# Weight preparation three chunks ahead instead of two, in the mixers of a two-layer block

## The chip, the core and the metric

The kernel runs on one core of a Trainium2 chip. The metric is the device time of one execution in microseconds (us), and the median of several executions is compared. The profile names the engines PE (TensorE matmul), PEld (its weight loads), DVE (VectorE), ACT (ScalarE), POOL (GpSimd) and SP (the engine that issues most DMA transfers).

## The reference

Two layers (`DEPTH = 2`) work on 256 tokens of width 1024. Each layer is a half FFN, a mixer and another half FFN, all in float32:

```python
for l in range(DEPTH):
    x = x + 0.5 * swiglu(rms_norm(x, norm_ffn1[l]), ffn1_wi[l], ffn1_wo[l])
    h = rms_norm(x, norm_mix[l])
    (u, q_raw, k_cmp, v_cmp, k_sel, v_sel, k_win, v_win,
     nsa_gate, gate_a, gate_b) = jnp.split(h @ w_in[l], SPLIT_POINTS, axis=-1)
    y_a = s5_branch(u, ...)            # a linear state-space scan over the tokens, then a gated product
    y_b = nsa_branch(q_raw, ...) @ nsa_w_up[l]   # attention over compressed, selected and window keys
    merged = jax.nn.sigmoid(gate_a) * y_a + jax.nn.sigmoid(gate_b) * y_b
    x = x + merged @ w_out[l]
    x = x + 0.5 * swiglu(rms_norm(x, norm_ffn2[l]), ffn2_wi[l], ffn2_wo[l])
```

The FFN's inner width is 2816. The columns of `w_in` are 512 for u, 512 for q, six groups of 128 for keys and values, 24 gate logits, and 1024 each for gate_a and gate_b.

## The kernel before, in words

**Weights come in chunks.** `plan` lists every chunk of weights of the whole program in the order of use, each 128 partitions by at most 1024 columns. A chunk is loaded into a buffer `raw` (four of them, `nr`), and then split: ScalarE writes a high part `whi` (L169 with the norm's gain as a scale, L349 without), and VectorE the low part `wlo` as the rest (L170, L349). There are four `whi` and four `wlo` buffers (`nh`). The chunks of `w_in`, which this text speaks of most, hold two blocks of 128 rows and are split in two halves, so two instructions on each engine for a chunk. Every product is made of three matmuls (`mm3`, L381 to L383): high by high, high by the activation's low part, low by high.

**How far ahead a split stands.** `next` hands out the next chunk and first calls `prepare` with a distance, `LA` = 2. `prepare` emits splits (and the loads that they need) until that many chunks beyond the one handed out are split:

```python
        while k.ns < min(k.nu + la, n):
```

Here `ns` counts the chunks split and `nu` those handed out.

**A mixer's work in order** (`mix`). A `gemm` makes a product of 256 tokens by up to 512 columns: two banks of PSUM with the tag `gu`, one for each half of the tokens (t), of which there are two in all; so the next `gemm` needs a bank that has been evacuated. The gemms are: u (512 columns, chunks in two pairs, each pair for both t), keys and values for the compression (384), the other keys and values with the gate logits (408), then two products with compression weights that stay in `raw` (L550 on the tile `kc`), q (512), four for the two gates (512 each, evacuated by a tanh at L1322), four with `ssm_w_glu`, two with `nsa_w_up`, and the output projection. The first evacuation of u is at L1282, and scales by the token's norm; VectorE transposes it (L1283), and the state-space branch starts from it (L550 on `ya` and `yb`, rotations at L933 to L941, the scan at L890, and the products with the state at L907). The evacuation of q is at L1049.

**The norm.** x is normed after the product: the hidden activations of the products are x itself, and each evacuation multiplies by the reciprocal root mean square. `norms` makes it, by a square with a running sum for each half of the tokens on ScalarE (L363) and two small steps on GpSimd. It is called behind the mixer's first gemm, and sets where ScalarE takes the two squares:

```python
        with k.tc.issue_after(k.hi_ins[k.ns - k.opt['SQ']].ins):
            k.rn = [k.rstd(t) for t in range(2)]
```

`SQ` is 1, so on ScalarE the squares stand behind the high part of the latest chunk that has been split. `hi_ins` holds each chunk's last high instruction.

**What sets the order.** The instructions are recorded in the order of the Python code, and a scheduler then sets each engine's own order by dependencies, free buffers, priorities and a model of the time. Each engine takes its instructions in that order. So a split that is emitted earlier moves other instructions around it on ScalarE, VectorE and TensorE.

Of the kernel before, what the change touches and what calls it, by code (L numbers as in the profile page):

```python
# [79 lines left out]
class Model:  # L80
    def __init__(k, tc, ctx, a, out, opt):
        k.tc, k.nc, k.a, k.out, k.opt = tc, tc.nc, a, out, opt
        e = ctx.enter_context
        k.pc = e(tc.tile_pool(name="const", bufs=1))
        k.pw = e(tc.tile_pool(name="weights", bufs=4))
        k.ps = e(tc.tile_pool(name="work", bufs=2))
        k.pp = e(tc.tile_pool(name="psum", bufs=1, space=PSUM))
        if not opt.get('auto', True):
            e(tc.manual_schedule())
        k.chunks, k.raw, k.hl, k.hi_ins = [], {}, {}, {}  # L90
        k.nd = k.ns = k.nu = k.held = 0
        k.bg, k.credit, k.budget = None, 0.0, 0.0
        k.fence, k.fence_n, k.late = (), 0, []
        k.steps = []


    def bank(k, shape=(128, 512), tag="tr", dtype=F32):
# [81 lines left out]
    def pull(k):  # L179
        k.credit = min(k.credit + k.budget, k.budget)  # L180
        while k.bg and k.credit > 0:
            cost = next(k.bg, None)
            if cost is None:
                k.bg = None
            else:
                k.credit -= cost

    def next(k, la=None):

        i = k.nu  # L190
        k.nu += 1
        if i and not k.chunks[i - 1][1]:
            k.held -= 1
        k.prepare(k.opt['LA'] if la is None else la)
        k.pull()
        return k.hl.pop(i)

# [1064 lines left out]
    def mix(k):  # L1262
# [2 lines left out]
        N = k.N  # L1265
        r4 = lambda dt=F32: k.sb([128, 1024], "r4", k.opt['n4'], dt)
        r8 = lambda: k.sb([128, 2048], "r8", k.opt['n8'])
        N['V'] = k.sb([128, 2, 2, 128], "V", 1)
        N['kT'] = k.sb([128, 2, 2, 2, 256], "kT", 1, F32R)
        ps = k.gemm(k.hstat, 8, 512, k.turns(k.opt['O2']))  # L1270
# [83 lines left out]
        def mm(kk, t, W, hs=(0, 1)):  # L1354
            for h in hs:
                cs = slice(h * 512, (h + 1) * 512)
                k.mm3(y[t, h], k.hstat(kk, t), (W[0][:, cs], W[1][:, cs]), kk == 0, kk == 7)

        for kk in range(5):
            W = k.next()  # L1360
            for t in range(2):
                mm(kk, t, W)
# [43 lines left out]
def hybrid_kernel(tc, out, opt, **a):  # L1406
    with ExitStack() as ctx:
# [3 lines left out]
_INS = ['x', 'norm_ffn1', 'ffn1_wi', 'ffn1_wo', 'norm_mix', 'w_in', 'ssm_lambda_re', 'ssm_lambda_im', 'ssm_log_dt',  # L1411
        'ssm_b_re', 'ssm_b_im', 'ssm_c_re', 'ssm_c_im', 'ssm_d', 'ssm_w_glu', 'q_norm', 'k_norm', 'cmp_pe', 'cmp_w1',
        'cmp_w2', 'nsa_w_up', 'w_out', 'norm_ffn2', 'ffn2_wi', 'ffn2_wo']
OPT = dict(nr=4, nh=4, LA=2, DLA=3, n1=10, n2=8, n4=7, n8=5, HP=2000, HN=2000, BG=1.2, FN=1, O1=22, WU=7, WV=7, SQ=1, LB=1, FB=2, O2=22, B1=1.0, B2=1.0)


# [17 lines left out]
```

## Time and profile before

| | us |
|---|---|
| median of 3 runs | 1166.65 (1166.4 to 1167.07) |
| the profiled execution | 1167.36 |
| its span, first to last instruction | 1165.6 |
| TensorE busy | 1153.3 (99% of the span) |
| VectorE busy | 827.1 (71%) |
| ScalarE busy | 671.9 (58%) |
| first mixer, 200.99 to 416.23 | 215.24 |
| second mixer, 779.03 to 991.47 | 212.44 |

The ends of matmuls are modelled and overlap the next matmul's start, so a busy TensorE says that something was always in flight, and the starts of the matmuls tell how fast they go. The two mixers are bounded here by the same two instructions of the program, the first update of x by the FFN ahead of them and a product at the same place of the FFN behind them.

### The profile page before, as it was taken

How to read it: one execution, taken by the hardware profiler on the slowest of the kernel's cores; microseconds unless marked ns; L12 is line 12 of the kernel's file. 1: busy time of each engine (PE TensorE's matmuls, PEld its weight loads, DVE VectorE, ACT ScalarE, POOL GpSimd, SP SyncE). 2: the span in 40 equal slices, each digit the busy share in tenths (PEclk: the TensorE clock that was granted, in tenths of full speed). 3: DMA queues.
4: the chain of work that ended last, by engine and by line, in shares of the span. 5: the costliest groups of instructions: out<-in, count | busy, mean ns of one | idle time of the engine just before them, and what ended most of it. 6: DMA issues, size and time to landing. Idle time of an engine off the chain costs nothing.

```text
span 1165.6 us, 17595 instructions
## 1 busy us (share of the span) xinstructions
PE 1153.3 (99%) x6148; PEld 939.7 (81%) x6148; DVE 827.1 (71%) x1578; ACT 671.9 (58%) x1176; POOL 96.0 (8%) x177
## 2 busy tenths in 40 slices
PE   9999999999999999999999999999999999999998
PEld 6888887877877888888888888788788778888886
DVE  5798597797776665555567986977987666655654
ACT  6755665646674565555566565555667646555552
POOL 3000000021032000000030000002112200000000
PEclk9999999999999999999999999999999999999999
DMA  8765646464443566665665555565654335766662
GB/s 239 232 193 166 186 144 209 124 204 141 155 118 106 174 206 191 187 183 185 192 181 184 181 179 169 157 178 158 200 162 145 109 110 170 227 184 185 191 183 88
DMA packets 150266, 200.40 MB, mean 172 GB/s; under 512 B 10145, under 2 KB 121025, under 8 KB 150177
## 3 DMA queue, kind: packets, MB, share of 16 engines
q1 hardware_dynamic: 148656, 196.93, 55.4%
q0 software_dynamic: 1136, 1.82, 0.8%
q8 instruction: 48, 0.79, 0.3%
q10 hardware_dynamic: 384, 0.52, 0.2%
q14 instruction: 42, 0.34, 0.1%
HBM read 198.18 MB, written 1.05 MB: 171 GB/s over the span
## 4 chain that ended last, share of the span: by engine, by line
PE 95%; DVE 3%; ACT 1%; issue 0%; POOL 0%; DVEq 0%; ACTq 0%; POOLq 0%
PE gu L381 20%; PE gu L383 20%; PE gu L382 20%; PE yb L382 4%; PE yb L383 4%; PE yb L381 4%; PE ya L383 4%; PE ya L381 4%; PE ya L382 4%; PE tr L496 2%; PE yb L1238 1%; PE yb L907 1%; PE tr L375 1%; PE tr L1227 1%; PE gu L448 1%; PE ya L1194 1%
## 5 line engine op out<-in xcount | busy, mean ns | idle before, releaser
L169 ACT ACTIVATE whi<-raw,gcol 128x512 fp32r<-128x512 f32 (+2 forms) x480 | 316.2, 710 | 197.8 <-PE gu L382 84.7
L170 DVE SCALAR_TENSOR_TENSOR wlo<-raw,gcol,whi 128x512 fp32r<-128x512 f32 (+2 forms) x480 | 335.6, 738 | 108.2 <-ACT whi L169 106.2
L381 PE MATMUL gu<-whi,hh 128*128 128x512 f32 (+2 forms) x944 | 373.5, 396 | 1.8 <-ACT r L1322 1.8
L383 PE MATMUL gu<-wlo,hh 128*128 128x512 f32 (+2 forms) x944 | 367.7, 393 | 0.0
L382 PE MATMUL gu<-whi,hl 128*128 128x512 f32 (+2 forms) x944 | 367.6, 389 | 0.0
L349 DVE TENSOR_TENSOR wlo<-raw,whi 128x1024 fp32r<-128x1024 f32 x128 | 156.5, 1225 | 120.0 <-ACT whi L349 117.2
L381 PEld LDWEIGHTS gu<-whi,hh 128*128 128x128 f32 x944 | 177.9, 188 | 36.3 <-ACT r L1322 2.6
L382 PEld LDWEIGHTS gu<-whi,hl 128*128 128x128 f32 x944 | 178.1, 189 | 34.8 <-issue 0.2
L383 PEld LDWEIGHTS gu<-wlo,hh 128*128 128x128 f32 x944 | 177.3, 188 | 34.8 <-issue 0.3
L349 ACT CAST whi<-raw 128x1024 fp32r<-128x1024 f32 x128 | 134.4, 1053 | 121.2 <-PE gu L382 102.4
L382 PE MATMUL yb<-whi,w1k 128*128 128x512 f32 x176 | 71.2, 406 | 0.2
L382 PE MATMUL ya<-whi,w1k 128*128 128x512 f32 x176 | 68.7, 392 | 0.0
L383 PE MATMUL yb<-wlo,w1k 128*128 128x512 f32 x176 | 68.1, 392 | 0.0
L381 PE MATMUL yb<-whi,w1k 128*128 128x512 f32 x176 | 68.0, 393 | 0.0
L381 PE MATMUL ya<-whi,w1k 128*128 128x512 f32 x176 | 67.6, 394 | 0.0
L383 PE MATMUL ya<-wlo,w1k 128*128 128x512 f32 x176 | 67.1, 390 | 0.0
L349 ACT CAST w1k<-tr 128x256 fp32r<-128x256 f32 x88 | 32.4, 368 | 43.5 <-PE tr L496 43.1
L513 DVE SCALAR_TENSOR_TENSOR w1k<-gu,rs,w1k 128x256 f32<-128x256 f32 x88 | 42.0, 479 | 16.8 <-ACT w1k L512 16.8
L512 ACT ACTIVATE w1k<-gu,rs 128x256 f32<-128x256 f32 x88 | 40.9, 467 | 18.4 <-PE gu L383 15.7
L356 POOL TENSOR_SCALAR rs<-ss 128x1 f32<-128x1 f32 (+3 forms) x22 | 6.8, 309 | 523.8 <-ACT w2k L363 472.3
L1217 POOL TENSOR_SCALAR w2k<-w2k,sm 128x128 f32<-128x128 f32 (+1 forms) x64 | 35.1, 568 | 103.8 <-DVE sm L1209 48.6
L349 DVE TENSOR_TENSOR w1k<-tr,w1k 128x256 fp32r<-128x256 f32 x88 | 36.6, 419 | 9.9 <-ACT w1k L349 9.8
(316 smaller groups left out, 1378.9 us busy)
## 6 DMA issues: line engine op xcount, KB each, us to landing
raw<-in_ffn_wi_dram SPq DMA_DIRECT2D x352, 256.0 KB, 3.3
raw<-in_ffn_wo_dram SPq DMA_DIRECT2D x88, 512.0 KB, 3.6
raw<-in_w_in_dram SPq DMA_DIRECT2D x48, 512.0 KB, 4.5
raw<-in_ssm_w_glu_dram SPq DMA_DIRECT2D x32, 256.0 KB, 3.0
raw<-in_w_out_dram SPq DMA_DIRECT2D x16, 512.0 KB, 3.7
raw<-in_cmp_w_dram SPq DMA_DIRECT2D x8, 512.0 KB, 4.9
raw<-in_nsa_w_up_dram SPq DMA_DIRECT2D x16, 256.0 KB, 4.0
raw<-in_w_in_dram SPq DMA_DIRECT2D x8, 408.0 KB, 4.2
```

Source lines behind the costliest of these rows:

```text
L169: k.hi_ins[i] = k.nc.scalar.activation(hi[:, s], r[:, s], AF.Copy, scale=c)
L170: k.lo_ins = k.nc.vector.scalar_tensor_tensor(lo[:, s], r[:, s], c, hi[:, s].bitcast(F32), op0=ALU.mult, op1=ALU.subtract)
L349: return k.nc.scalar.copy(hi, src), k.nc.vector.tensor_sub(lo, src, hi.bitcast(F32))
L375: m = k.nc.tensor.transpose(b[:, i], src[:, i * 128:(i + 1) * 128], k.id)
L381: mm(ps, a[0], b[0], start=first, stop=False)
L382: mm(ps, a[1], b[0], start=False, stop=False)
L383: return mm(ps, a[0], b[1], start=False, stop=last)
L448: last[2] = k.nc.tensor.matmul(ps[t], stat(kk, t)[a], W[i][b][:, cs[j]], start=kk == 0 and a + b == 0 and j == 0, stop=kk == nk - 1 and (a ...
L496: nc.tensor.transpose(b[:, i], act[t][:, i * 128:(i + 1) * 128], k.id)
L512: m = nc.scalar.activation(sg, ps[t][:, :256], AF.Silu, scale=r[t])
L513: nc.vector.scalar_tensor_tensor(a, ps[t][:, 256:], r[t], sg, op0=ALU.mult, op1=ALU.mult)
L1217: G.tensor_scalar(w[:, i], p[:, i], cf[:, j:j + 1], 0.0, op0=ALU.mult, op1=ALU.add)
```

## The change

The distance of `next` becomes a variable of the model. It is 3 (`LM`) from the start of a mixer to the output projection, and 2 everywhere else. The numbers of buffers stay, and so do `norms`, `gemm` and `prepare`.

```diff
@@ -92,6 +92,7 @@
         k.steps = []
+        k.la = opt['LA']
@@ -191,7 +192,7 @@
-        k.prepare(k.opt['LA'] if la is None else la)
+        k.prepare(k.la if la is None else la)
         k.pull()
         return k.hl.pop(i)
@@ -1265,6 +1266,7 @@
         r8 = lambda: k.sb([128, 2048], "r8", k.opt['n8'])
+        k.la = k.opt['LM']
         N['V'] = k.sb([128, 2, 2, 128], "V", 1)
...
         ps = k.gemm(k.hstat, 8, 512, k.turns(k.opt['O2']))
@@ -1356,6 +1358,7 @@
+        k.la = k.opt['LA']
         for kk in range(5):
             W = k.next()
@@ -1411,7 +1414,7 @@
-OPT = dict(nr=4, nh=4, LA=2, DLA=3, n1=10, n2=8, n4=7, n8=5, HP=2000, HN=2000, BG=1.2, FN=1, O1=22, WU=7, WV=7, SQ=1, LB=1, FB=2, O2=22, B1=1.0, B2=1.0)
+OPT = dict(nr=4, nh=4, LA=2, LM=3, DLA=3, n1=10, n2=8, n4=7, n8=5, HP=2000, HN=2000, BG=1.2, FN=1, O1=22, WU=7, WV=7, SQ=1, LB=1, FB=2, O2=22, B1=1.0, B2=1.0)
```

The lines of the changed kernel have moved by one to three numbers. SP's order of loads stays as it was.

**ScalarE at the start of the first mixer.** The 512-column splits are the second pair of u's chunks, the 384-column splits the chunks of the product behind it, L363 (now L364) the two squares, L1282 (now L1284) the two evacuations of u. Before:

```order
L169 ACTIVATE whi<-raw,gcol 128x512 x4
L349 CAST hh<-tr 128x4x128 x2
L169 ACTIVATE whi<-raw,gcol 128x384 x4
L363 ACTIVATE w2k,ss<-x 128x1024 x2
L1282 ACTIVATE w2k<-gu,rs 128x512
L169 ACTIVATE whi<-raw,gcol 128x384 x4
L1282 ACTIVATE w2k<-gu,rs 128x512
```

And with the change:

```order
L170 ACTIVATE whi<-raw,gcol 128x512 x4
L350 CAST hh<-tr 128x4x128 x2
L170 ACTIVATE whi<-raw,gcol 128x384 x6
L364 ACTIVATE w2k,ss<-x 128x1024 x2
L170 ACTIVATE whi<-raw,gcol 128x384 x2
L1284 ACTIVATE w2k<-gu,rs 128x512 x2
```

The two instructions of the third 384-column chunk have moved from behind the first evacuation to ahead of the squares, and those of the fourth to ahead of the first evacuation. The second mixer's rows read the same.

**TensorE behind the compression's products in the first mixer.** `r_2786` and `r_2787` (now `r_2794` and `r_2795`) are the two parts of the state, `r_1535`, `r_1614` and `r_1615` matrices that were made earlier, and the `gu` products the first of q. Before:

```order
L550 MATMUL ya<-kc_1851,raw 64x33 x64
L907 MATMUL yb<-r_1535,r_2320 64x128 x2
L907 MATMUL yb<-r_1614,r_2786 64x128 x2
L907 MATMUL yb<-r_1535,r_2320 64x128
L907 MATMUL yb<-r_1615,r_2787 64x128 x2
L907 MATMUL yb<-r_1535,r_2320 64x128
L381 MATMUL gu<-whi,hh 128x512
L382 MATMUL gu<-whi,hl 128x512
```

And with the change:

```order
L551 MATMUL ya<-kc_1851,raw 64x33 x64
L908 MATMUL yb<-r_1535,r_2328 64x128 x2
L382 MATMUL gu<-whi,hh 128x512
L383 MATMUL gu<-whi,hl 128x512
L382 MATMUL gu<-whi,hh 128x512
L383 MATMUL gu<-whi,hl 128x512
L908 MATMUL yb<-r_1614,r_2794 64x128 x2
L908 MATMUL yb<-r_1615,r_2795 64x128 x2
L908 MATMUL yb<-r_1535,r_2328 64x128 x2
L384 MATMUL gu<-wlo,hh 128x512
```

Four products of q's first chunk now stand ahead of the products with the state.

**ScalarE at the evacuation of q's second half in the first mixer.** L1322 (now L1324) evacuates a gate's bank, L1049 (now L1050) q's. Before:

```order
L1322 ACTIVATE r_2947<-gu,rh 128x512
L1002 ACTIVATE nr_2757<-tr 32x64
L169 ACTIVATE whi<-raw,gcol 128x512 x8
L1322 ACTIVATE r_2947<-gu,rh 128x512
L349 CAST kct<-tr 128x2x16
L1049 ACTIVATE w2k<-gu,rs 128x512
L1064 ACTIVATE w2k<-w2k 128x512
```

And with the change:

```order
L1324 ACTIVATE r_2955<-gu,rh 128x512
L350 CAST kct<-tr 128x2x16
L1050 ACTIVATE w2k<-gu,rs 128x512
L1065 ACTIVATE w2k<-w2k 128x512
L170 ACTIVATE whi<-raw,gcol 128x512 x8
L1324 ACTIVATE r_2955<-gu,rh 128x512
```

The evacuation of q's second half has moved from behind the eight high halves and the second gate evacuation to ahead of both.

## Rows read from the trace of the kernel before

**Rows 1.** The page: busy time of each engine, share, instructions.

```profile
PE 1153.3 (99%) x6148; PEld 939.7 (81%) x6148; DVE 827.1 (71%) x1578; ACT 671.9 (58%) x1176; POOL 96.0 (8%) x177
```

**Rows 2.** Windows, both mixers: us, busy us of PE, PEld, DVE, ACT, POOL, clock, DMA.

```profile
200.99:416.23 215.24, 211.52 (x1356) 173.17 (x1355) 158.51 (x282) 130.73 (x264) 35.24 (x65) 0.99 0.48 146
779.03:991.47 212.44, 210.65 (x1356) 173.22 (x1355) 159.03 (x282) 130.74 (x264) 33.05 (x62) 0.99 0.49 148
```

**Rows 3.** Waits of TensorE, whole span: us in total, times, longest us.

```profile
PE yb L907 <- DVE r L936: 3.1, 2, 1.5
PE gu L381 <- ACT r L1322: 1.8, 2, 1.3
```

**Rows 4.** Timeline of TensorE at both mixers' start: start us, us, instruction, [idle before].

```profile
215.84 0.39 PE L382 MATMUL gu<-whi,hl 128*128 128x512 f32 x1
...
217.44 0.39 PE L383 MATMUL gu<-wlo,hh 128*128 128x512 f32 x1
217.67 0.34 PE L381 MATMUL gu<-whi,hh 128*128 128x384 f32 x1
217.85 0.33 PE L382 MATMUL gu<-whi,hl 128*128 128x384 f32 x1
...
795.69 0.34 PE L381 MATMUL gu<-whi,hh 128*128 128x384 f32 x1
```

**Rows 5.** Timeline of ScalarE at both mixers' start.

```profile
212.15 1.12 ACT L169 ACTIVATE whi<-raw,gcol 128x384 fp32r<-128x384 f32 x2 [0.25 <-PE gu L382]
213.18 1.04 ACT L363 ACTIVATE w2k<-x 128x1024 bf16<-128x1024 f32 x1
...
215.28 0.69 ACT L1282 ACTIVATE w2k<-gu,rs 128x512 f32<-128x512 f32 x1
216.32 1.12 ACT L169 ACTIVATE whi<-raw,gcol 128x384 fp32r<-128x384 f32 x2 [0.34 <-PE gu L382]
...
794.34 1.12 ACT L169 ACTIVATE whi<-raw,gcol 128x384 fp32r<-128x384 f32 x2 [0.34 <-PE gu L382]
```

**Rows 6.** Timeline of VectorE in the first mixer.

```profile
219.42 0.71 DVE L1283 STREAM_TRANSPOSE r<-w2k 128x512 f32<-128x512 f32 x1
...
234.14 0.69 DVE L934 TENSOR_TENSOR w2k<-yb,r 128x512 f32<-128x512 f32 x1 [1.33 <-PE yb L550]
...
248.53 0.74 DVE L170 SCALAR_TENSOR_TENSOR wlo<-raw,gcol,whi 128x512 fp32r<-128x512 f32 x1
```

**Rows 7.** Timeline of TensorE, its three waits in the first mixer.

```profile
246.63 1.70 PE L907 MATMUL yb<-r,r 128*64 128x128 f32 x12 [1.54 <-DVE r L936]
...
271.28 0.51 PE L381 MATMUL gu<-whi,hh 128*128 128x512 f32 x1 [0.55 <-ACT r L1322]
...
278.88 0.50 PE L381 MATMUL gu<-whi,hh 128*128 128x512 f32 x1 [1.27 <-ACT r L1322]
```

**Rows 8.** Timeline of ScalarE: q's first chunk, the gate evacuations, both mixers.

```profile
245.88 1.34 ACT L169 ACTIVATE whi<-raw,gcol 128x512 fp32r<-128x512 f32 x2 [3.95 <-DMA raw<-in_w_in_dram]
...
272.75 5.50 ACT L169 ACTIVATE whi<-raw,gcol 128x512 fp32r<-128x512 f32 x8 [1.43 <-PE gu L382]
278.16 0.67 ACT L1322 ACTIVATE r<-gu,rh 128x512 f32<-128x512 f32 x1
...
278.80 0.70 ACT L1049 ACTIVATE w2k<-gu,rs 128x512 f32<-128x512 f32 x1
...
853.53 0.66 ACT L1049 ACTIVATE w2k<-gu,rs 128x512 f32<-128x512 f32 x1
...
855.32 0.67 ACT L1322 ACTIVATE r<-gu,rh 128x512 f32<-128x512 f32 x1
```

**Rows 9.** Windows around the two L907 waits and the L1322 waits.

```profile
244.00:252.00 8.00, 6.32 (x69) 4.53 (x66) 7.74 (x20) 6.09 (x11) 1.99 (x2) 0.79 0.80 264
822.00:830.00 8.00, 6.45 (x66) 4.99 (x63) 7.74 (x20) 6.06 (x11) 1.99 (x2) 0.79 0.82 270
...
270.00:280.00 10.00, 8.18 (x37) 6.01 (x36) 8.16 (x19) 7.85 (x14) 2.70 (x5) 1.00 0.34 91
```

## The prediction

> **What bounds the kernel now.** The page's first table comes first: TensorE is busy for 1153.3 of 1165.6 us [rows 1]. Next, the busy time of each mixer, from the first update of x by the FFN before it to the product at the same place of the FFN behind it: the first takes 215.24 us with 211.52 busy, the second 212.44 with 210.65 [rows 2]. The two run the same number of products, so 3.72 and 1.79 us of idle time are all that a better order could give back, apart from the clock. The table of waits names them [rows 3]: 3.1 us of L907 for the state written at L936, once in each mixer, and 1.8 us of a product bank for its evacuation at L1322, twice, both in the first mixer [rows 7]. Nothing else on TensorE waits inside the mixers, so everywhere else the matmul order is the path, and a wait that the change puts before a product counts in full. The mixer's start is such a place: the last product of u (512 columns) issues at 217.44, the first of the 384-column product behind it at 217.67, with no gap, and the second mixer does the same at 795.69 [rows 4].
>
> **The change, part by part.** I use u0 to u3 for the four chunks of the first product, k0 to k3 for those of the second. No instruction is added or removed; splits move, and with them what stands behind them in their engines' order.
>
> *The norm and the evacuation at the mixer's start.* `norms` hangs the two squares (L363) behind the latest high half. With two chunks ahead that is k1, with three it is k2; the order shows it. In before, k0 and k1 find free buffers, the squares start at 213.18 and the evacuation of the first u bank (L1282) at 215.28, while k2 starts only at 216.32 [rows 5]. It can't start sooner: there are four high buffers, u2 holds the one that k2 gets, and the second half's last product with u2's high part issues at 215.84 and takes 0.39 [rows 4]. In the new order ScalarE stands before k2 from 213.18 to 216.32 with the squares behind it. Then come k2 (1.03 us from its start to the next instruction, as k1's 212.15 to 213.18), the two squares with their sums (213.18 to 215.28, 2.10 us), k3 (1.03 again) and the evacuation itself (0.69) [rows 5]: 216.32 + 1.03 + 2.10 + 1.03 + 0.69 = 221.17. TensorE sees it 0.05 later, as at 278.16 + 0.67 to 278.88 [rows 7, 8]: 221.22. The two product banks both hold u, so the 384-column product can't begin before. It began at 217.67: **3.55 us** of new wait. In the second mixer k2 starts at 794.34, the bank comes free at 799.24, and 795.69 was the old start [rows 4, 5]: 3.55 again. Sum **+7.10**. The second evacuation follows at once and is done near 221.8, some 3 us before the second bank is asked for (20 products of 0.17 later, [rows 4]); the transpose of u on VectorE (0.71, [rows 6]) is done near 222.6, and its products, which now stand 23 products in, at about 225.2. Neither adds.
>
> *Does the rest of the mixer absorb the delay?* Behind the wait TensorE is 3.55 us late, and the chain that ends in L907's wait could have caught up. It doesn't: VectorE stands 1.33 us for TensorE's second state product before the rotation at 234.14 [rows 6], that product keeps its place in the order, and all of the scan comes behind it. So the chain moves with TensorE. I take 0 back.
>
> *The wait before L907.* TensorE waits 1.54 us until 246.63 for the state [rows 7]. Now the first q products stand in front of the state products, and they need a high half that ScalarE makes from 245.88, after 3.95 us for the weights to land; half of 1.34 brings it to 246.55 [rows 8]. The same moment: 0. The weights are asked for when the compression's products give a load buffer back, so this moves with TensorE too. Behind it, the low half of that chunk is done at 248.53 + 0.74 = 249.27 [rows 6]; TensorE gets there with four products (0.23 each) and six state products, which took 1.70 us here at a lowered clock [rows 7], so at 249.25. At the full clock it would be some 0.9 us earlier and wait that long. Bounds 0 and +0.9 for each mixer; I take 0, since the clock was low here both times [rows 9].
>
> *The two waits for L1322.* In the first mixer ScalarE takes four chunks of high halves from 272.75 on, 5.50 us, before the second gate evacuation at 278.16; only then comes the evacuation of the second q bank (L1049, 278.80) [rows 8]. So one bank alone carries the gate products, and TensorE waits 0.55 and 1.27 us [rows 7]. In the second mixer L1049 (853.53) stands ahead of the second L1322 (855.32) [rows 8], and neither wait is there [rows 3]. The new order puts it ahead in both mixers. Bounds 0 and -1.82; I take the second mixer's behaviour: **-1.82**, in the first mixer alone.
>
> *The clock behind the new wait.* [...] Waits of 0.55 and 1.27 us among dense products left it at the full level (the waits at 271.28 and 278.88, [rows 7]; the window that holds both shows 1.00, [rows 9]). The new wait lies among dense products too, but is 2.8 times the longest that left the clock alone, and more than twice the one that didn't. Bounds 0 and 1.68 in each mixer. I take 1.4, near the upper: part of the slow stretch may fall into the wait itself, where it costs nothing. Sum **+2.8**. [...]
>
> 7.10 - 1.82 + 2.8 = +8.1 us. Against the profiled execution's own 1167.36 that is 1175.4; its span was 1165.6, and the median of the runs, 1166.65, lies 0.71 below it. The forecast for the median is 1174.7.
>
> **The rivals.**
> - *No low clock behind the wait.* The waits of 1.27 us and less among dense products speak for it, the length of the new one against. 1174.7 - 2.8 = 1171.9.
> - *More waits than counted.* The first mixer's two stay (+1.82), or new ones arise, as the 0.9 us before the low half in each mixer: up to 3.6 us more, 1178.3. For it: VectorE is at 7.74 of 8 us around L907 [rows 9], and its order changes all through the attention. Against: outside the named places TensorE never waited in either mixer, though their orders already differ.
> - *The delay is given back at L907.* If the scan's chain doesn't move with TensorE but with VectorE's own earlier work, the 1.54 us wait and the low clock behind it go in both mixers: 2 x (1.54 + 1.68) = 6.4, and 8.1 - 6.4 = +1.7: 1168.3. The 1.33 us at 234.14 speaks against it; it decides once that wait is gone.
> - *Not slower: k2 doesn't wait.* If a high buffer is free for k2 at 213.2, the evacuation moves only by two chunks' halves, 2 x 1.03, to 215.28 + 2.06 + 0.69 + 0.05 = 218.08, and each mixer loses 0.41 us, too little to bring the clock down. With 1.82 saved: 0.82 - 1.82 = -1.0, 1165.6. It decides at a loss below 0.91 us for each mixer. Against it: in before k2 waited for TensorE at 216.32 for the same buffer [rows 5].
>
> **How the numbers follow.** About 0.2% (2.3 us) is what a measurement of this kernel can tell from no change. Chances: the forecast 0.60, its own range 1172.8 to 1176.6 (the clock's term from 0.9 to 3.36 and the low half's wait of up to 1.4 in both together); no low clock 0.15; more waits 0.16; given back at L907 0.05; k2 free 0.04. The range takes the first three in: 1171.0 to 1178.5, and leaves out some 0.15: the last two and a tail of the third. The last two lie within 0.2%, apart from 0.02 below it: faster 0.02, same 0.07, slower 0.91.
>
> **What would show it.** Right: on ScalarE the squares of the mixer start about 1 us behind k2's start and not behind k1; TensorE has a wait of some 3.5 us on L1282 before the first 384-column product, once in each mixer; the clock is below 1.00 in the microseconds behind it; the L907 place still waits some 1.5 us, now for a high half; no wait for L1322 in the first mixer; both mixers take the same time within 1 us. The FFNs keep theirs. Wrong: no wait at L1282 (the first step), a full clock behind it (the last), a shorter wait before L907, or waits inside the attention that no row of before has.

## The result, and the profile after

The changed kernel takes 1174.28 us (median of four executions, 1172.73 to 1175.11), beside 1166.86 (1166.40 to 1167.87) for the kernel before on the same chip: a ratio of 1.0068, 95% interval 1.0056 to 1.0080. Forecast were 1174.7, in a range of 1171.0 to 1178.5, and 0.91 for slower. The profiled execution took 1174.21, its span 1172.4, 6.8 us more than that of before.

The page's first line, the answer to [rows 1], shows the same work and nearly the same busy time. What has grown is TensorE's standing, from 12.3 to 18.8 us.

```profile
PE 1153.6 (98%) x6148; PEld 942.1 (80%) x6148; DVE 827.7 (71%) x1578; ACT 670.7 (57%) x1176; POOL 93.8 (8%) x177
```

TensorE's waits after, beside [rows 3]: those for L907 and for the gate evacuation are gone, and three others have come, each once in each mixer. L1284 is the evacuation of u, L170 a high half, L1050 the evacuation of q.

```profile
PE gu L382 <- ACT w2k L1284: 6.6, 2, 3.3
PE gu L382 <- ACT whi L170: 3.0, 2, 1.5
PE gu L382 <- ACT w2k L1050: 2.1, 2, 1.0
```

Each mixer is best cut in two at the compression's thin products (L550, now L551). The windows of before, start to cut and cut to end, in the columns of [rows 2]:

```profile
200.99:240.91 39.92, 39.78 (x308) 34.66 (x306) 29.51 (x45) 20.50 (x42) 6.08 (x15) 1.00 0.43 126
240.91:416.23 175.32, 171.73 (x1049) 138.51 (x1049) 128.99 (x238) 110.23 (x223) 29.16 (x50) 0.99 0.50 151
779.03:818.95 39.92, 39.79 (x310) 34.68 (x308) 29.54 (x45) 20.50 (x42) 6.08 (x15) 1.00 0.44 125
818.95:991.47 172.52, 170.87 (x1049) 138.53 (x1049) 129.49 (x238) 110.24 (x223) 26.97 (x47) 0.99 0.50 153
```

And of after, between the same instructions:

```profile
201.22:246.35 45.13, 41.68 (x309) 36.22 (x307) 29.31 (x45) 20.26 (x42) 5.91 (x15) 0.96 0.39 111
246.35:418.42 172.07, 169.47 (x1049) 138.04 (x1049) 129.66 (x238) 110.01 (x223) 27.28 (x50) 0.99 0.50 153
781.17:826.30 45.13, 41.68 (x308) 36.26 (x306) 29.28 (x45) 20.22 (x42) 5.91 (x15) 0.96 0.40 111
826.30:998.37 172.07, 169.44 (x1049) 138.02 (x1049) 129.71 (x238) 110.06 (x223) 26.99 (x47) 0.99 0.50 153
```

The first part grows by 5.21 us in both mixers. The rest shrinks, by 3.25 us in the first and 0.45 in the second, and both mixers now take 217.20. The sum is 2 x 5.21 - 3.25 - 0.45 = 6.72 of the span's 6.8, so the FFNs keep their time. (Between the medians the rise is 7.42; the account below goes by the two profiled executions.)

**The start.** ScalarE after, beside [rows 5]:

```profile
212.36 1.12 ACT L170 ACTIVATE whi<-raw,gcol 128x384 fp32r<-128x384 f32 x2 [0.25 <-PE gu L383]
216.53 1.12 ACT L170 ACTIVATE whi<-raw,gcol 128x384 fp32r<-128x384 f32 x2 [3.04 <-PE gu L383]
217.56 1.04 ACT L364 ACTIVATE w2k<-x 128x1024 bf16<-128x1024 f32 x1
...
219.63 1.11 ACT L170 ACTIVATE whi<-raw,gcol 128x384 fp32r<-128x384 f32 x2
220.64 1.24 ACT L1284 ACTIVATE w2k<-gu,rs 128x512 f32<-128x512 f32 x2
```

These are k1, k2, the first of the two squares, k3 and the evacuations. ScalarE stands 3.04 us ahead of k2 with the squares behind it. TensorE, beside [rows 4], first and second mixer:

```profile
217.65 0.40 PE L384 MATMUL gu<-wlo,hh 128*128 128x512 f32 x1
221.37 0.69 PE L382 MATMUL gu<-whi,hh 128*128 128x384 f32 x1 [3.32 <-ACT w2k L1284]
...
797.61 0.40 PE L384 MATMUL gu<-wlo,hh 128*128 128x512 f32 x1
801.33 0.49 PE L382 MATMUL gu<-whi,hh 128*128 128x384 f32 x1 [3.32 <-ACT w2k L1284]
```

From the last product of u to the next it is 3.72 us instead of 0.23: 3.49 lost. The other 1.72 of the first part's 5.21 are the clock, whose granted share is 0.72 in the 6 us that begin some 1.4 us ahead of the product's start:

```profile
220.00:226.00 6.00, 4.63 (x18) 4.64 (x19) 2.38 (x4) 1.89 (x4) 1.35 (x4) 0.72 0.42 130
800.00:806.00 6.00, 4.67 (x18) 4.68 (x19) 2.38 (x4) 1.85 (x4) 1.31 (x4) 0.72 0.40 125
```

6 x 0.28 = 1.68 us at full speed are missing there: the share is 0.50 from 222 to 224 and from 802 to 805, and 1.00 in the microsecond from 225 and in that from 805.

### The profile page after: what moved, and what is told of

It is laid out like the page before. It is cut to its first block, busy times and chain, and to the rows that moved or that the text cites. A ratio compares the mean times of both kernels' runs of the same rounds, so it can differ in the third digit from the quotient of the medians.

```text
span 1172.4 us, 17606 instructions
## 1 busy us (share of the span) xinstructions
PE 1153.6 (98%) x6148; PEld 942.1 (80%) x6148; DVE 827.7 (71%) x1578; ACT 670.7 (57%) x1176; POOL 93.8 (8%) x177
## 3 DMA queue, kind: packets, MB, share of 16 engines
q0 software_dynamic: 1136, 1.82, 0.8%
## 4 chain that ended last, share of the span: by engine, by line
PE 93%; DVE 4%; ACT 1%; issue 1%; POOL 0%; DVEq 0%; ACTq 0%; POOLq 0%
PE gu L382 20%; PE gu L384 19%; PE gu L383 19%; PE yb L383 4%; PE yb L384 4%; PE yb L382 4%; PE ya L384 4%; PE ya L382 4%; PE ya L383 4%; PE tr L497 2%; PE yb L1239 1%; PE tr L376 1%; PE gu L449 1%; PE ya L1195 1%; PE tr L1228 1%; DVE wlo L171 1%
## 5 line engine op out<-in xcount | busy, mean ns | idle before, releaser
L170 ACT ACTIVATE whi<-raw,gcol 128x512 fp32r<-128x512 f32 (+2 forms) x480 | 315.4, 709 | 205.7 <-PE gu L383 82.6
L1218 POOL TENSOR_SCALAR w2k<-w2k,sm 128x128 f32<-128x128 f32 (+1 forms) x64 | 31.6, 514 | 112.3 <-ACT w2k L1202 70.9
```

Of the source, the lines that this page charges most:

```text
L170: k.hi_ins[i] = k.nc.scalar.activation(hi[:, s], r[:, s], AF.Copy, scale=c)
L1218: G.tensor_scalar(w[:, i], p[:, i], cf[:, j:j + 1], 0.0, op0=ALU.mult, op1=ALU.add)
```

## The experiments

All times are medians; the ratios are to executions of the kernel before beside them on the same chip, whose medians were 1166.68 us for the first four, 1166.75 for the next four, 1166.17 for the last two.

### Is it the distance, or what hangs on it?

**same_anchor**: three chunks ahead, but the squares hung where they were.

```diff
-    def norms(k):
+    def norms(k, sq=None):
-        with k.tc.issue_after(k.hi_ins[k.ns - k.opt['SQ']].ins):
+        with k.tc.issue_after(k.hi_ins[k.ns - (sq or k.opt['SQ'])].ins):
...
-        k.norms()
+        k.norms(2)
         k.r = k.rn
```

> The change, but with the mixer's two squares hung behind the high half that stands one chunk further back (k1 again instead of k2). Theory (the place of the squares is all that costs): ScalarE, VectorE and TensorE then read in the order of the kernel before, so 1166.9 within 1 us, no wait for u's evacuation at the mixer's start, and the two waits of 0.55 and 1.27 us for the gate evacuation are back in the first mixer. Rival (three chunks ahead cost by themselves, as high buffers and loads are taken a chunk earlier): 1170 or more, and a wait for u's evacuation of over 1 us stays.

Measured: 1166.48, ratio 1.0001 (0.9992 to 1.0011), and the waits of [rows 3] are back:

```profile
PE yb L908 <- DVE r L937: 3.1, 2, 1.5
PE gu L382 <- ACT r L1324: 1.8, 2, 1.3
```

**first_gemm_only**: three chunks ahead for one product only.

```diff
         k.norms()
+        k.la = k.opt['LA']
         k.r = k.rn
```

> Three chunks ahead for the mixer's first product alone, up to the squares; two from there on. Theory (all of the change comes from the squares behind k2): the time of the changed kernel, 1174.3 within 1.5 us, with all its waits: 3.3 us for u's evacuation, 1.0 us for q's first half, none for the gate evacuation in the first mixer. Rival (the distance in the rest of the mixer carries part of it): under 1172.5, or the waits in the attention as before (L907 on VectorE, two on the gate evacuation).

Measured: 1174.30, ratio 1.0061 (1.0046 to 1.0076), with the changed kernel's waits (6.6 us for u's evacuation, 2.9 for a high half, 2.1 for q's), two short ones beside them in the second mixer (0.7 for a low half and 0.4) and a low clock behind u's evacuation in both mixers (0.72 in the 6 us from 221 and in those from 801).

On every engine the first of these kernels has the order of before, instruction for instruction, and the second that of the changed kernel. So a split that is emitted a chunk earlier changes, by itself, nothing anywhere in the mixer; the scheduler puts it where it stood, and it is not so, as was said ahead of the result, that an earlier split moves the instructions around it. The whole change is the two squares behind k2 instead of k1, with what the scheduler makes of that further on. The rival, that the distance costs by itself, falls.

### How long a wait, and what does the clock do behind it?

**stall_1400**: squares behind k1, and u's evacuation behind k3.

```diff
-        k.norms()
+        k.prepare(4)
+        k.norms(3)
...
+            with k.tc.issue_after(k.hi_ins[k.ns - 1].ins):
-            S.activation(u.rearrange("p a c -> p (a c)"), ps[t], AF.Copy, scale=k.r[t])
+                S.activation(u.rearrange("p a c -> p (a c)"), ps[t], AF.Copy, scale=k.r[t])
```

(`norms` as in same_anchor.)

> Squares behind k1 as before, but the first evacuation of u behind k3. ScalarE starts k2 at 216.32 and k3 1.03 later, so the evacuation ends at 216.32 + 2 x 1.03 + 0.69 = 219.07 and TensorE waits some 1.45 us instead of the changed kernel's 3.5; the order behind it is nearly the changed kernel's. Theory (a wait of this length leaves the clock alone, as those of 1.27 us and less did): no low clock in the first 10 us of the 384-column product, 1174.3 - 2 x (2.05 + 1.65) = 1166.9. Rival (any wait at this place brings the clock down): a low stretch stays in both mixers, 1174.3 - 2 x 2.05 = 1170.2.

Measured: 1167.00, ratio 1.0002 (0.9992 to 1.0011). TensorE's wait, the same in both mixers (the second is shown), and the clock around it in each:

```profile
796.25 0.45 PE L382 MATMUL gu<-whi,hh 128*128 128x384 f32 x1 [1.60 <-ACT w2k L1286]
```

```profile
217.00:223.00 6.00, 4.40 (x24) 3.85 (x23) 3.53 (x6) 3.13 (x6) 0.18 (x2) 1.00 0.64 202
795.00:801.00 6.00, 4.75 (x28) 4.50 (x28) 2.38 (x4) 1.77 (x4) 0.00 (x0) 1.00 0.49 141
```

**stall_2500**: the changed kernel, with k3's split (the next one that is emitted) behind u's first evacuation.

```diff
-            S.activation(u.rearrange("p a c -> p (a c)"), ps[t], AF.Copy, scale=k.r[t])
+            m = S.activation(u.rearrange("p a c -> p (a c)"), ps[t], AF.Copy, scale=k.r[t])
+            if t == 0:
+                k.fence, k.fence_n = (m,), 1
```

> The changed kernel, but with k3's halves behind the first evacuation of u, so that only k2 and the squares stand ahead of it: 216.32 + 1.03 + 2.10 + 0.69 = 220.14, a wait of some 2.5 us. Theory by step one of the prediction: each chunk ahead of the evacuation is worth its 1.03 us, and the low clock stays, as the wait is still twice the longest that left it alone: 1174.3 - 2 x 1.0 = 1172.3. Rival (the clock stays up below 3 us): 1174.3 - 2 x (1.0 + 1.65) = 1169.0. Second rival (the squares are what is waited for, k3 hides beside them): 1174.3, wait still 3.5.

Measured: 1170.71 (five executions, 1168.28 to 1171.61), ratio 1.0032 (1.0019 to 1.0045). The wait is the same in both mixers, but the clock behind it isn't:

```profile
220.19 0.45 PE L382 MATMUL gu<-whi,hh 128*128 128x384 f32 x1 [2.35 <-ACT w2k L1284]
...
798.85 0.45 PE L382 MATMUL gu<-whi,hh 128*128 128x384 f32 x1 [2.35 <-ACT w2k L1284]
```

```profile
220.00:226.00 6.00, 5.81 (x24) 5.82 (x25) 2.37 (x4) 1.72 (x4) 0.80 (x3) 0.72 0.38 121
798.00:804.00 6.00, 5.15 (x30) 5.15 (x31) 2.37 (x4) 2.38 (x6) 1.26 (x6) 1.00 0.48 138
```

The waits follow the sum of the prediction (1.45 and 2.5 expected, 1.60 and 2.35 found): k3 is worth 3.32 - 2.35 = 0.97 us, the squares 3.32 - 1.60 = 1.72, where the sum had 1.03 and 2.10. (In stall_1400 k3 stands 0.25 us for a buffer of its own, so the squares' price comes out too low there.) The clock stayed at 1.00 behind both waits of 1.60, fell behind one of the two of 2.35 (0.72 and 1.00 in the windows above), and behind both of 3.32 (0.72). So neither theory for stall_2500 holds for both mixers, and its time lies between the two.

**filled_start**: does the standing bring the clock down? The changed kernel, with products into a free bank that nobody reads.

```diff
+    def fill(k, n, tag='tr'):
+        b = k.bank((128, 512), tag)
+        for _ in range(n):
+            m = k.nc.tensor.matmul(b, k.hh[:, 0, :128], k.hh[:, 0:2].rearrange("p a b -> p (a b)"), start=True, stop=True)
+        return m
...
+        with k.tc.issue_after(k.mm.ins):
+            k.fill(14)
         k.norms()
```

> The change, with 14 products of 512 columns that nobody reads put on TensorE behind u's last product (14 x 0.229 = 3.2 us), so that it works through most of the wait instead of standing. The start of the 384-column product stays where the changed kernel has it. Theory (the standing brings the clock down): full clock behind it in both mixers. Behind q the first mixer has before's order again, with its two waits for the gate evacuation, so 1166.7 + 2 x 3.5 = 1173.7. Rival (the clock falls at this place for another reason, such as the squares or the loads): the low stretch stays in both mixers, 3.3 more: 1177.0.

Measured: 1173.49 (1173.38 to 1173.72), ratio 1.0060 (1.0046 to 1.0074). TensorE in the first mixer, and the window of each:

```profile
217.70 3.38 PE L370 MATMUL tr<-hh 128*128 128x512 f32 x14
221.19 0.44 PE L388 MATMUL gu<-whi,hh 128*128 128x384 f32 x1
```

```profile
217.00:223.00 6.00, 5.89 (x28) 4.81 (x27) 3.53 (x6) 4.72 (x9) 2.32 (x7) 1.00 0.48 142
797.00:803.00 6.00, 5.89 (x26) 4.54 (x25) 2.52 (x5) 5.12 (x10) 2.32 (x7) 1.00 0.61 200
```

The next product starts within 0.2 us of where it does in the changed kernel, and the clock is 1.00 behind it in both mixers, where the changed kernel has 0.72. So it is the standing, and not the squares or the loads, that costs the second part. The time is that of before and two starts, 1166.75 + 2 x 3.49 = 1173.73, since the rest of this kernel has before's waits again.

### Is it k2's wait for a buffer?

**k2_own_buffer**: k2 is the seventh chunk of a mixer; it gets tiles of the tag `w2k`, and stands where it stands with the change. `Pair` hands out the tile that a half lies in.

```diff
+        k.alt = k.nu + 6
...
+        if i == k.alt:
+            hi, lo = (Pair([k.sb([128, 512], "w2k", k.opt['n2'], F32R) for _ in range(2)]) for _ in range(2))
+        else:
-        hi = k.pw.tile([128, 1024], F32R, name="whi", bufs=k.opt['nh'])
-        lo = k.pw.tile([128, 1024], F32R, name="wlo", bufs=k.opt['nh'])
+            hi = k.pw.tile([128, 1024], F32R, name="whi", bufs=k.opt['nh'])
+            lo = k.pw.tile([128, 1024], F32R, name="wlo", bufs=k.opt['nh'])
```

> The change, with a buffer of its own for k2 in each mixer (four tiles of the tag w2k in place of a whi and a wlo), so that it needn't wait for u2's products; the squares still stand behind k2. Theory (step one: the wait of k2 for a high buffer is what makes the stall, the halves and squares by themselves fit in): k2 at 213.2, squares to 216.3, k3 from u2's buffer to 217.35, evacuation to 218.04, a wait of 0.4 us in each mixer instead of 3.5, and no low clock there: 1165.6 to 1167.7, by whether the waits of 1.0 us for q's first half stay. Rival (the squares behind one more chunk are late by themselves): a wait of over 2 us stays, 1171 or more.

Measured: 1165.02, ratio 0.9985 (0.9976 to 0.9994), faster than before. ScalarE at the first mixer's start:

```profile
214.16 1.13 ACT L182 ACTIVATE w2k<-raw,gcol 128x384 fp32r<-128x384 f32 x2 [0.67 <-DMA raw<-in_w_in_dram]
...
...
218.28 0.67 ACT L1297 ACTIVATE w2k<-gu,rs 128x512 f32<-128x512 f32 x1
```

With its own buffer k2 starts 2.37 us earlier than with the change; what it waits for now is its weights, which have only just landed. TensorE waits 0.95 us in the first mixer, 1.7 in both together (0.4 in each were expected), and nowhere for the gates or for q. This is the rival "k2 doesn't wait", made true by hand: 1165.6 was worked out for it. The buffer is the cause of the stall. That the kernel is faster than before is not the wait alone: TensorE's busy time is 1151.9 us, 1.4 less than before, since the order behind has moved too.

### The other low stretch, and versions faster than before

**before_filled_L907**: the kernel before with `fill(6, 'gu')` behind the last of the compression's thin products.

```diff
+            if kv:
+                with k.tc.issue_after(m0.ins):
+                    k.fill(6, 'gu')
             pb = k.sb([128, 1], "pb", 2)
```

(`m0` is the last product of the loop above it.)

> The kernel before, with 6 products of 512 columns that nobody reads (1.4 us) behind the compression's thin products, where TensorE stands 1.54 us for the state. Theory (the standing there brings the clock down, and each low stretch costs about 1 us): no low stretch in either mixer, every execution at the granted clock 1.000, which in before's own executions goes with 1165.4: 1165.4, narrow. Rival (the thin products ahead of it bring it down): low stretches stay in some executions, median 1166.7 or more.

Measured: 1164.18, ratio 0.9981 (0.9972 to 0.9990), the fastest of all. In its profiled execution the clock is 1.00 through both mixers. TensorE behind the thin products:

```profile
244.58 1.65 PE L369 MATMUL gu<-hh 128*128 128x512 f32 x6
246.16 0.72 PE L914 MATMUL yb<-r,r 128*64 128x128 f32 x8
246.82 0.50 PE L387 MATMUL gu<-whi,hh 128*128 128x512 f32 x1
...
249.13 0.50 PE L389 MATMUL gu<-wlo,hh 128*128 128x512 f32 x1 [0.78 <-DVE wlo L170]
```

With the clock at 1.00 (0.79 around L907 in [rows 9]) TensorE comes earlier to q's first low half and waits 0.78 us for it. The two waits for the gate evacuation are gone too, because the order behind has moved, so the 2.6 us are not the clock's alone. The theory is met in part: there is no low stretch in the profile, but three of the eleven executions show 0.999, and the time is 1.2 us under the one expected.

**q_evacuated_first**: the kernel before, with the next split hung behind the evacuation of q's second half.

```diff
-        nc.scalar.activation(src.rearrange("p h d -> p (h d)"), ps, AF.Copy, scale=k.r[t])
+        m = nc.scalar.activation(src.rearrange("p h d -> p (h d)"), ps, AF.Copy, scale=k.r[t])
+        if t:
+            k.fence, k.fence_n = (m,), 1
```

> The kernel before, with the next chunk's split that is emitted behind the evacuation of q's second half hung behind that evacuation, in both mixers. Theory (the first mixer's two waits for the gate evacuation come from q's second bank being evacuated behind eight high halves): both waits go, 1166.7 - 1.8 = 1164.9, to 1164.4 with the slow start behind each wait. Rival (the high halves are then late for the gates' products): other waits of the same size, 1166.7 or more.

Measured: 1180.43, ratio 1.0119 (1.0103 to 1.0135): a miss for both, far more than the rival's time. The wait that it was to remove is smaller in total, and others have come, the longest of 2.2 us once in each mixer:

```profile
PE tr L1115 <- DVE kb L1108: 4.4, 2, 2.2
...
PE gu L381 <- ACT r L1324: 1.4, 2, 0.7
```

All waits together are 5.6 us more than before's. And the clock falls behind both of the new ones of 2.2 us, to 0.79 in the 8 us around the first and 0.72 in 12 us around the second: 8 x 0.21 + 12 x 0.28 = 5.0 us at full speed (the profiled execution's mean is 0.993, before's 0.997). The two make up most of the 11.3 us by which the span is longer.

**both_6** and **both_7**: k2_own_buffer with `fill(6, 'gu')` and `fill(7, 'gu')` as in before_filled_L907.

> The change with k2's own buffers and, in each mixer, 6 unread products of 512 columns behind the compression's thin products. Theory (the two effects add): 1165.0 less what the low stretches behind L907 cost there, about 1 us each and two in most executions, and less the standing that the fill covers nothing of: 1163.3, granted clock 1.000 nearly always. Rival (with the clock up, TensorE is earlier at the low half of q's first chunk and waits there instead, and the order behind brings the gate's waits back): 1165 or more.

> As the run with 6, with 7 unread products. Theory: the seventh takes 0.23 us out of the wait for q's first low half in each mixer and costs nothing: the same time as with 6 within 0.5 us. Rival (TensorE has no idle time left there): 0.5 us more than with 6.

Measured: 1171.71, ratio 1.0050 (1.0036 to 1.0063), and 1171.99, 1.0050 (1.0038 to 1.0063). The clock was nearly full (0.998 to 1.000 in all ten executions), and yet the two gains didn't add. The waits with 6:

```profile
PE tr L1055 <- DVE w1k L1035: 2.0, 3, 0.8
...
PE gu L400 <- ACT whi L182: 1.5, 1, 1.5
...
PE gu L400 <- ACT w2k L1069: 1.0, 1, 1.0
```

The fill made the scheduler move the middle of the mixer. The waits for the state (2.7 us in k2_own_buffer) are gone, but TensorE now waits ahead of the transposes of the keys, for a high half and for q, and k2_own_buffer had none of these waits. Its busy time is 1155.1 us (k2_own_buffer 1151.9), its idle time 14.8 (11.9): the unread products came on top, and what they filled came back elsewhere. The theory of both_6 fails; the rival's time holds, but not its reason, since the gate's waits stay away and the low half is waited for in one mixer alone, 0.7 us. The seventh product changes the time by 0.3 us, as expected, but again with other waits (q twice, 2.1 us).

## Why the prediction was right, step by step

| step | forecast | measured |
|---|---|---|
| wait for u's evacuation | 2 x 3.55 | 2 x 3.49 |
| low clock behind it | 2 x 1.4 | 2 x 1.72 |
| the rest of the first mixer | -1.82 | -3.25 |
| the rest of the second mixer | 0 | -0.45 |
| sum | +8.1 | +6.72 |

**The norm and the evacuation.** Right in mechanism and size. That the buffer of k2 makes the stall was shown by giving it another, that the chunks and squares behind it have nearly the prices of the sum by the two shorter waits.

**The clock.** Right. The clock fell behind both waits in the profile of the changed kernel and behind both in that of first_gemm_only (0.72 in 6 us each time), against the rival without a low clock; filled_start, with 1.00 at the same place, shows that the standing is the cause. The 1.4 of the sum was an estimate under the bound of [rows 9], 8 x 0.21 = 1.68 us, and no run shows it: the size is the bound itself, 1.68 by the clock and 1.72 by what is left of the first part's growth. Next to nothing of the slow stretch falls into the wait: the share is still 1.00 until 221.3 and 801.5, and the products start at 221.37 and 801.33. So the waits of 3.32 us were paid a second time by the products behind them, one of the two of 2.35 too, and neither of those of 1.60.

**The rest absorbs nothing of the delay.** Right: at the L907 place TensorE stands 1.51 us, now for a high half, until 252.03, which is 5.40 later than in [rows 7]; the thin products ahead are 5.44 later.

**L907.** Right: no wait for the low half where the clock is down (0.79 in the 8 us from 249 and in those from 829), and nearly the one worked out for the full clock (0.9 us) where it was up. In the second mixer of first_gemm_only, with the changed kernel's order, the clock stayed at 1.00 at this place:

```profile
834.64 0.50 PE L384 MATMUL gu<-wlo,hh 128*128 128x512 f32 x1 [0.74 <-DVE wlo L171]
```

Only the sum for the lowered clock was too short. It took the four products of q at 0.23 us each, the full speed; they took 2.01 us (252.03 to 254.04, at a granted clock of 0.50), so TensorE came to the low half some 1 us after it was done, and not at the same moment. The 0.78 us in before_filled_L907 belong to another order.

**The waits for the gate evacuation.** Right: gone in the first mixer, as the second had it.

**What was mis-sized is the rest of the mixer**, twice, and the errors partly cancel. The wait of 1.0 us in each mixer for the first half of q was not foreseen; it is the rival "more waits than counted", and a wait inside the attention that no row of before has, which the prediction itself named as a sign of being wrong. Counted from the compression's thin products, TensorE comes to q's last product 2.4 us earlier than before (19.6 us behind them, not 22.0), since state products that stood ahead of it now stand behind, while the evacuation starts 0.5 us later. On ScalarE it stands behind casts of the keys that wait for VectorE:

```profile
265.00 0.36 ACT L350 CAST kT<-tr 64x256 fp32r<-64x256 f32 x1 [2.06 <-DVE kT L350]
...
266.77 0.37 ACT L350 CAST kT<-tr 64x256 fp32r<-64x256 f32 x1 [0.66 <-DVE kT L350]
...
268.06 0.68 ACT L1050 ACTIVATE w2k<-gu,rs 128x512 f32<-128x512 f32 x1
```

Against it stands something that the prediction didn't price at all: the busy time of the rest fell by 2.26 us in the first mixer and 1.43 in the second, for the same products. The groups by line show most of it in the thin ones; the attention's and the state's products of the first mixer, before:

```profile
L1238 PE MATMUL yb<-w2k,V 128*64 128x128 f32 x96 | 8.1, 282 | 0.0
L907 PE MATMUL yb<-r,r 128*64 128x128 f32 x96 | 8.0, 295 | 1.7 <-DVE r L936 1.5
```

And after:

```profile
L1239 PE MATMUL yb<-w2k,V 128*64 128x128 f32 x96 | 7.2, 280 | 0.0
L908 PE MATMUL yb<-r,r 128*64 128x128 f32 x96 | 7.2, 296 | 0.0
```

They stand in other groups among the other products, and their sum is 1.7 us less. One such place, before:

```profile
263.18 0.88 PE L907 MATMUL yb<-r,r 128*64 128x128 f32 x12
263.99 0.44 PE L1035 MATMUL tr<-id,w1k 128*128 128x128 f32 x2
264.36 0.43 PE L907 MATMUL yb<-r,r 128*64 128x128 f32 x2
```

And after, 22 of them in one run, without transposes between:

```profile
266.26 1.52 PE L908 MATMUL yb<-r,r 128*64 128x128 f32 x22
```

By the starts of the single products (those written 128x128 in the rows), the step from one with 128*64 weights to one with 128*128, or back, takes 0.20 us; between two of the first it is 0.06 on average, between two of the second 0.11. The rest of the first mixer had 19 such steps before and has 11 now, the second 15 and 11. By these prices that is an estimated 0.7 to 1.1 us in the first mixer and 0.4 to 0.6 in the second, a part of the 2.26 and 1.43. What makes up the rest was not found, and no run tested the order of the thin products by itself. The clock is no rival here: the rest of each mixer shows 0.99 before and after.

The step that failed is thus "the rest of the mixer absorbs nothing" taken as "its own time stays", and with it the sentence that idle time is all that a better order could give back. The order moved all through the attention, and I took that for risk on one side only. Against the forecast the rest has 1.81 us more idle time and 3.69 less busy time. That the median came out within 0.5 us of the forecast is partly luck: two sizes of opposite sign that were not priced, and a clock term that was 0.6 us too small in both mixers together.

## What to carry to other kernels

Before a look-ahead distance is changed, ask what else reads the counter that it moves: here the splits themselves stayed where they were, and an anchor that named "the latest split" carried the norm behind a chunk that waits for a buffer. Ask also whether a stall on the busiest engine is paid twice: here one of 3.32 us was paid at its length, and again, with 1.72 us, by the slow products behind it, while the clock stayed at 1.00 behind one of 1.60. Unread products kept the clock up (1.00 in filled_start, where the changed kernel has 0.72), but those of before_filled_L907 and both_6 also moved the order. And in a kernel whose order a scheduler sets, a local fix is worth what the whole new order is worth: two changes that gained 1.7 and 2.6 us gave a loss of 5.5 together.

## What was not expected of the hardware

The times of the kernel before fall into three groups. Its 21 executions beside the second four runs, by the mean granted clock of each:

| clock | executions | us |
|---|---|---|
| 1.000 | 4 | 1165.10 to 1165.73 |
| 0.999 | 8 | 1165.90 to 1166.83 |
| 0.997 | 9 | 1167.01 to 1167.67 |

The profile of before has the clock at 0.79 around L907 in both mixers [rows 9] and a mean of 0.997; that of same_anchor, with the same order, has it in the second alone, a mean of 0.999, and 1165.86 us. So each low stretch there goes with about 1 us of the whole time. At the place itself it is more: from the end of L907's wait to the first low-half product TensorE takes 5.22 us in the profile of before (246.63 to 251.85, low) and 3.70 in that of same_anchor (247.03 to 250.73, full), 1.52 less in the same order; where the difference goes was not found. And the low stretch doesn't always come: behind the same wait of 1.5 us, and in stall_2500 behind the same 2.35, it comes in one mixer and not in the other, while in q_evacuated_first it comes behind both waits of 2.2. What decides that, these runs don't show. With the standing filled ten of eleven executions were within 1163.83 to 1164.68, though three showed 0.999; the eleventh took 1166.20 at 1.000, so the clock isn't all that varies.
